# A decoder step of two layers: diagonal squares of 16, turned values through DRAM, halves on GpSimd

## The chip, the core and the metric

One core of a Trainium2 chip runs one program: TensorE (PE, with its weight loads PEld), VectorE (DVE), ScalarE (ACT), GpSimd (POOL) and SyncE (SP, which issues all DMAs of this kernel). The metric is device microseconds of one execution, lower is better. All arithmetic is in float32, or in float32 split into a high and a low half of a faster matmul type (fp32r).

## The reference

One step of a hybrid recurrent decoder with two layers, on 1024 prompt tokens and 8 sample rows, with model width 1024. Each layer normalises `x`, projects it with one wide weight matrix, mixes along time, and projects back:

```python
h = RMSNorm(x) * (1 + scale) + shift          # scale, shift, gate from silu(c) @ ada_w + ada_b
proj = h @ w_in
# even layer: 8 heads of gated DeltaNet (DK = DV = 128) beside 8 heads of mLSTM
#   o_a solves, per chunk, (I + A) U = rhs with A strictly lower triangular
# odd layer: 4 heads of GLA beside 4 heads of retention (DK = 128, DV = 256), per chunk:
#   o     = (q * decay) @ S + att @ v          # att: masked, decayed q k^T
#   S_new = decay * S + (k * decay)^T @ v
y = concat(branch outputs) * silu(z)
x = x + gate * (y @ w_out)
```

After both layers comes a plain RMSNorm. Outputs are `y` of both groups and the final states.

## The kernel before

**Recording and planning.** The kernel does not run its instructions in the order of its code. `Recorder` takes each call as an `Op` with its queue, a cost (`_cost` for DVE, ACT and POOL, `_pe_cost` for PE) and its dependencies; `order` then plans all queues, forwards from the ranks of the code and backwards in turns, and `emit` issues each queue's instructions in that order. Every engine works in order, and SP too: a DMA that waits for something holds those behind it. `self.nc.after` adds a dependency to all that is recorded while it is set; `urgent` puts what it encloses earlier. All instructions carry the line of `emit`, L451, in the profile, so they are told apart by their tiles.

**Layout.** Activations lie with features on partitions and 1032 tokens (1024 and 8) along the free side, in `slot` buffers with fixed names (`s_kd`, `s_vs`, `s_EM`, `s_pt` and so on in the profile). Small things lie in one `arena` that the even and the odd layer use in turn, from the same offsets. Weights come 128 columns at a time (`load_w`: 512 KB into `wf`, two buffers) and `halves` splits them: ACT writes `whi`, DVE writes the difference `wlo`. A projection of one such tile is 3 token blocks x 8 row tiles x 3 products (high x high, high x low, low x high), 72 matmuls of 344 columns.

**Even layer.** For each of eight heads, `gdn_proj` projects k, v, z and q, `gdn_mix` turns and scales them and walks over eight chunks of 128 tokens, and a generator of the mLSTM heads is advanced in between. For each head `inverse` computes the inverse of eight unit triangular matrices of 128x128 (the chunks'): it sends the diagonal 32x32 blocks through DRAM (`nd`), so that all diagonal 8x8 squares lie on 128 partitions, substitutes there in seven steps of two DVE operations, sends the result back through DRAM (`yd`) as blocks of 32 (`D`), and doubles twice: from 8 to 16 and from 16 to 32. Each doubling has two blocks of 32 small matmuls (8 chunks x 4 partition groups), a masking operation by `icode` between them, a subtraction and a DVE transpose. Doublings from 32 to 64 and to 128 follow. `even_setup` lays down `icode`, the unit squares `i8` and zeros in `yd`.

**Between the layers.** `out_proj` multiplies the 16 tiles of y by the output weights; `split` loads a y tile from DRAM (`yd`) into a staging slot and makes its halves, on ACT and then on DVE or POOL. The last two, 14 and 15, are split after the first output columns have been begun on the other 14. `odd_setup` loads the odd layer's constants (`lmask`, `rdm`, `rin`, `rend`, `w2`, `cosT`, `sinT`).

**Odd layer.** For each of four heads: `gla_proj`, `gla_mix`, `ret_proj`, `ret_mix`. Both mixes need keys and values with tokens on partitions. `by_token` turns one 128x1024 tile with 16 DVE transposes of 32x256, each from one group of 32 partitions to another; `v_tokens` does that for the two value tiles of a head (into `s_kd` and `s_vs`), and each mix does it once more for its keys (into `s_N`). `chunks256` then walks over the eight chunks: per chunk the values are weights of two matmuls against `aT` and the moving side of two against the keys. `finish256` squares and norms the result (a small sum through `rd` in DRAM, back on all partitions), multiplies by the gate on DVE and by the norm on POOL, and stores y. After the last head, `out_proj` runs once more and ends in the final norm.

Of the kernel before, what the change touches and what calls it, by code (L numbers as in the profile page):

```python
# [9 lines left out]
F32 = mybir.dt.float32  # L10
F32R = mybir.dt.float32r
AF = mybir.ActivationFunctionType
ALU = mybir.AluOpType
# [4 lines left out]
T = 1024  # L18
# [6 lines left out]
NC = T // L  # L25
# [14 lines left out]
def host_constants():  # L40
    f = np.float32
    c = {}
    c["ident"] = np.eye(128, dtype=f)
    pos = np.concatenate([np.arange(T), np.full(NS, 8192)]).astype(f)
    inv = (f(10000.0) ** (-np.arange(64, dtype=f) / f(64))).astype(f)
    ang = (pos[None, :] * inv[:, None]).astype(f).astype(np.float64)
    c["cosT"] = np.concatenate([np.cos(ang), np.cos(ang)], 0).astype(f)
    c["sinT"] = np.concatenate([np.sin(ang), -np.sin(ang)], 0).astype(f)
    lg = np.log(1.0 - 2.0 ** (-5.0 - np.arange(4)))
    s, t = np.arange(L)[:, None], np.arange(L)[None, :]  # L50
    dm = np.zeros((L, 4, L))
    for h in range(4):
        dm[:, h, :] = np.where(t >= s, np.exp(lg[h] * np.maximum(t - s, 0)), 0.0)
    c["rdm"] = dm.astype(f).reshape(L, 4 * L)
    inn = np.exp(lg[:, None] * (np.arange(L)[None, :] + 1.0))
    c["rin"] = np.broadcast_to(inn[None], (128, 4, L)).astype(f).reshape(128, 4 * L).copy()
    c["rend"] = np.exp(lg[None, :] * (L - 1.0 - np.arange(L)[:, None])).astype(f)
    lm = np.zeros((32, 6, 32), f)
    ss, tt = np.arange(32)[:, None], np.arange(32)[None, :]
    for i, m in enumerate((16, 8, 4, 2, 1)):  # L60
        lm[:, i, :] = (ss // (2 * m) == tt // (2 * m)) & (ss % (2 * m) < m) & (tt % (2 * m) >= m)
    lm[:, 5, :] = ss == tt
    c["lmask"] = np.tile(lm, (4, 1, 1)).reshape(128, 192).copy()

    code = np.zeros((32, 32), f)
    for i in range(2):
        code[lm[:, 1 - i, :].T > 0] = 1.0 + i
    c["icode"] = np.tile(code, (4, 1))
    c["i8"] = np.tile(np.eye(8, dtype=f).reshape(1, 64), (128, 1))

    sel = np.zeros((2, 4, 8, 4, 32), f)
    for to, at in enumerate((1, 0, 2, 3)):
        for i in range(8):
            sel[:, at, i, to, i] = 1.0
    c["sel"] = sel.reshape(64, 128)
    return c
# [32 lines left out]
def _cost(queue, method, out, args, kw):  # L109

    n, sbuf, psum, scalars = _operands(out, args, kw)
    if queue == "scalar":
        return (165 + 0.84 * n if psum else 207 + 0.832 * n) + 60 * (scalars > 0) + 60 * ("accum_out" in kw), False
    if queue == "vector":
        if method == "tensor_reduce":
            return 150 + 1.042 * _elems(args[1]), False
        if method == "reciprocal":
            return 150 + 6.25 * n, False
        if method == "transpose":
            return 436.0, False  # L120
        if method == "tensor_tensor_scan":
            return 160 + 2.083 * n, True
        if method == "memset":
            return 65 + 0.52 * n, False
        if method in ("tensor_copy", "tensor_scalar") and not psum:
            return 152 + 0.57 * n + 45 * (scalars > 0), True
        return 153 + 1.042 * n + 57 * (scalars > 0), not psum
    if queue == "gpsimd":
        if kw.get("op") == ALU.pow:
            return 150 + 186.0 * n, True  # L130
        if method == "memset":
            return 100 + 0.83 * n, False
        if method == "tensor_copy":
            return 100 + 1.12 * n, True
        return (195 + 2.15 * n if method == "tensor_tensor" else 250 + 0.83 * n), True
    return 0.0, False


def _pe_cost(method, out, args, kw):
# [3 lines left out]
    n, rows, cols = _elems(kw["rhs"]), kw["lhsT"].shape[0], kw["lhsT"].shape[1]  # L143
    if kw["rhs"].dtype == F32R:
        return 0.45 * n + 2.5, "pass"
    if kw.get("tile_position") is not None and cols <= 32:
        return (max(1.87 * n / 4, 15.0) if rows > 32 else 15.0), (rows, cols)
    if rows <= 64 and cols <= 64:
        return max(1.67 * n + 9, 117.0), (rows, cols)
    kind = "whole" if rows == 128 and (cols == 128 or kw.get("tile_position") is None) else (rows, cols)  # L150
# [316 lines left out]
class Step:  # L467
# [428 lines left out]
    def halves(self, w, n=KT):  # L896
        hi, lo = (self.wtile(x, [128, KT, 128])[:, 0:n] for x in ("whi", "wlo"))
        self.act(hi, w[:, 0:n], AF.Copy)
        self.nc.vector.tensor_tensor(lo, w[:, 0:n], hi, op=ALU.subtract)
        return hi, lo  # L900

    def proj_parts(self, parts, ks):
# [390 lines left out]
    def inverse(self, N):  # L1293
# [3 lines left out]
        nd, yd = (self.nyd[x][self.turn(x, 2)] for x in ("nd", "yd"))  # L1297
        by32 = lambda x, j: x.rearrange("(c j q) x -> c j (q x)", c=NC, j=4)[:, j, 0:1024].rearrange(
            "c (s t) -> s c t", t=32)
        by8 = lambda x: x[:, 0:256].rearrange("m (r t) -> m r t", t=32)[:, :, 0:8]  # L1300
        blocks = [slice(32 * j, 32 * j + 32) for j in range(4)]
        for j, b in enumerate(blocks):
            dma(by32(nd, j), N[b, :, b])
        n8, y8, t8 = (self.const([128, 8, 8], x) for x in ("n8", "y8", "t8"))
        dma(n8, by8(nd))
        G.tensor_copy(y8, self.i8)
        for s in range(7):
            n = 7 - s
            V.tensor_tensor(t8[:, 0:s + 1, 0:n], y8[:, 0:s + 1, s:s + 1].to_broadcast([128, s + 1, n]),
                            n8[:, s:s + 1, s + 1:8].to_broadcast([128, s + 1, n]), op=ALU.mult)  # L1310
            V.tensor_tensor(y8[:, 0:s + 1, s + 1:8], y8[:, 0:s + 1, s + 1:8], t8[:, 0:s + 1, 0:n], op=ALU.subtract)
        dma(by8(yd), y8)

        t = self.slot("EM", name="inv")
        D, At, qt, Dt = (t[:, 256 * i:256 * i + 256].rearrange("p (c t) -> p c t", c=NC) for i in range(4))
        for j, b in enumerate(blocks):
            dma(D[b], by32(yd, j))
        V.transpose(Dt, D)
        for i in range(1, 3):
            p = self.ps(None, [128, NC, 32])  # L1320
            for c in range(NC):
                for j, b in enumerate(blocks):
                    self.mm(p[b, c, :], N[b, c, b], Dt[b, c, :], tile_position=(32 * j, 32 * j))
            V.scalar_tensor_tensor(At, self.icode.unsqueeze(1).to_broadcast([128, NC, 32]), float(i), p,
                                   op0=ALU.is_equal, op1=ALU.mult)
            p = self.ps(None, [128, NC, 32])
            for c in range(NC):
                for j, b in enumerate(blocks):
                    self.mm(p[b, c, :], At[b, c, :], D[b, c, :], tile_position=(32 * j, 32 * j))
            V.tensor_tensor(D, D, p, op=ALU.subtract)  # L1330
            V.transpose(Dt, D)
        Y = self.slot("Y", [128, NC, L], name="Y")
        G.memset(Y, 0.0)
        for b in blocks:
# [2 lines left out]
        p = self.ps(None, [128, 2, NC, 32])  # L1337
# [283 lines left out]
    def even_setup(self):  # L1621
        nc, a, V, G = self.nc, self.a, self.nc.vector, self.nc.gpsimd
        self.bkq = self.const([128, 258], "bkq")
        G.memset(self.bkq, 0.0)
        self.icode = self.const([128, 16], "icode").bitcast(mybir.dt.bfloat16)
        self.i8 = self.c_load("i8", [128, 8, 8])
        zero = self.slot("aT", [128, 264], name="zero")
        G.memset(zero, 0.0)
        for x in self.nyd["yd"]:
            self.nc.sync.dma_start(x, zero)  # L1630
        code = self.slot("EM", [128, 32], name="code")
        self.nc.sync.dma_start(code, self.a["icode"])
        self.nc.vector.tensor_copy(self.icode, code)
        self.vs = self.const([128, 2, NS], "mvs")
        self.ozs = self.const([128, 2, NS], "mozs")
        self.nms = self.const([128, 2, 2, NS], "mnms")
# [22 lines left out]

    def odd_setup(self):  # L1660
        nc, a = self.nc, self.a
        self.lmask = self.c_load("lmask", [128, 6, 32])
        self.rdm = self.c_load("rdm", [128, 4, L])
        self.rin = self.c_load("rin", [128, 4, L])
# [5 lines left out]
        nc.sync.dma_start(self.cosT, a["cosT"])  # L1670
        self.sinT = self.slot("mk", name="sinT")
        nc.sync.dma_start(self.sinT, a["sinT"])
        self.glr = self.slot("va", name="glr")
        self.qk_w = [self.load_w(a["od_w_in"][0], c) for c in (0, 512)]

# [32 lines left out]
    def by_token(self, out, x):  # L1708

        x = x[:, 0:T].rearrange("p (c t) -> p c t", t=L)  # L1710
        for i in range(0, 128, 32):
            for j in range(0, 128, 32):
                self.nc.vector.transpose(out[j:j + 32, :, i:i + 32], x[i:i + 32, :, j:j + 32])

    def v_tokens(self, v):
        vt = []
        for i, tag in enumerate(("kd", "vs")):
            t = self.slot(tag, [128, NC, 128], name="vt")
            self.by_token(t, v[i])
            vt.append(t)  # L1720
        return vt

    def chunks256(self, aT, qg, kt, vt, decay, out):

# [222 lines left out]
    def out_proj(self, src, l, mod):  # L1947
# [45 lines left out]
        def x_in(n):  # L1993
            x = xs[n % 2] if last else self.x_slot(n)
            nc.sync.dma_start(x, self.xd[l][n])
            return x
# [57 lines left out]
            G.tensor_tensor(wl[:, 1], w, wl[:, 0], op=ALU.subtract)  # L2054
        for k in late:
            split(k)
        x2 = [x_in(n) for n in range(2)]
        for n in range(2):
            for j in range(3):
# [61 lines left out]
    def build(self):  # L2121
        tc, nc = self.tc, self.nc
        with ExitStack() as ctx:
# [20 lines left out]
            self.sd = [dr.tile([16, 128], F32, name=f"sd{i}") for i in range(2)]  # L2144
            self.spd = dr.tile([16, W], F32, name="spd")
            self.rd = [dr.tile([4, QB], F32, name=f"rd{i}") for i in range(2)]
            self.nyd = {x: [dr.tile([128, 264], F32, name=f"{x}{i}") for i in range(2)] for x in ("nd", "yd")}
            self.program()
            with tc.manual_schedule():
                self.nc.emit()  # L2150
# [103 lines left out]
```

## Time and profile before

| | |
|---|---|
| median of three runs | 2292.83 us (2287.20 to 2294.88) |
| the profiled execution | 2289.05 us, its span 2287.0 us |
| mean granted clock of PE | 0.987 |
| busy: PE, DVE, ACT, POOL | 2221.4, 1382.8, 747.7, 527.7 us |
| moved by DMA | 235.20 MB |

The span is the time from the first to the last instruction of the program in the profiled execution; the time of the execution has 2.05 us more around it. A busy time is the union of an engine's instructions, so matmuls that overlap in the pipeline count once. The even layer's heads run until about 1160 us, the odd layer's projections begin at about 1400 us, and the last output projection ends the span.

### The profile page before, as it was taken

The page shows a single profiled execution, that of the slowest core. Times are in us where ns is not written, and L with a number is a line of the kernel's source. Part 1 is how long each engine was busy: PE and PEld are TensorE (multiplying, and loading weights), DVE is VectorE, ACT ScalarE, POOL GpSimd, SP SyncE. Part 2 cuts the span into 40 slices and gives each one's busy share as a digit, 9 for nine tenths or more (in the row PEclk, how much of TensorE's full clock was granted, in tenths as well). Part 3 has the DMA queues.
Part 4 walks back from the last instruction along what each step waited for, and adds up shares of the span by engine and source line. Part 5 has one row for each costly group of instructions (what it writes and reads, how often), then busy time and mean ns, then how long its engine had stood idle before and what let it go on. Part 6 is the DMA issues. An engine that isn't in the chain of part 4 may idle for free.

```text
span 2287.0 us, 44726 instructions
## 1 busy us (share of the span) xinstructions
PE 2221.4 (97%) x18844; PEld 2070.0 (91%) x18844; DVE 1382.8 (60%) x2700; ACT 747.7 (33%) x1374; POOL 527.7 (23%) x385
## 2 busy tenths in 40 slices
PE   6999999999999999999989999999999999998998
PEld 5777788899999999899989999999999999997997
DVE  6774646565564646556453355876976876977332
ACT  4422323232233233232331134234225324334322
POOL 3121112111123012211330031422422422433100
PEclk8999999999999999999999999999999999998999
DMA  9362544422143212432362221233142143246222
GB/s 260 124 165 60 152 133 121 129 77 72 40 118 105 69 52 86 108 95 72 114 216 84 75 76 38 56 122 107 43 136 94 50 133 95 56 149 209 74 58 91
DMA packets 285455, 235.20 MB, mean 103 GB/s; under 512 B 47819, under 2 KB 257733, under 8 KB 285246
## 3 DMA queue, kind: packets, MB, share of 16 engines
q1 hardware_dynamic: 285254, 232.35, 34.6%
q8 instruction: 147, 2.41, 0.4%
q14 instruction: 54, 0.44, 0.1%
HBM read 185.59 MB, written 46.91 MB: 102 GB/s over the span
## 4 chain that ended last, share of the span: by engine, by line
PE 88%; DMA 4%; DVE 4%; issue 1%; ACT 1%; POOL 1%; SPq 1%; POOLq 0%; DVEq 0%; ACTq 0%
PE pj L451 68%; PE A L451 14%; PE B L451 6%; DMA wf<-in_ev_w_in 1%; SPq L451 1%; DMA s_aT<-rd 0%; DVE s_h L451 0%; DMA s_h<-in_x_prompt 0%; DVE arena L451 0%; DVE s_N L451 0%; DMA s_pt<-yd 0%; DVE s_pt L451 0%; DMA ed<-s_Y 0%; DMA s_mp<-gd 0%; DVE s_mp L451 0%
## 5 line engine op out<-in xcount | busy, mean ns | idle before, releaser
L451 PE MATMUL pj<-s_h,whi 128*128 128x344 f32 (+1 forms) x6024 | 1498.6, 327 | 10.8 <-ACT s_h L451 5.4
L451 PEld LDWEIGHTS pj<-s_h,whi 128*128 128x128 f32 (+1 forms) x6024 | 1042.7, 189 | 44.8 <-issue 25.3
L451 PE MATMUL pj<-s_h,wlo 128*128 128x344 f32 (+1 forms) x3024 | 982.2, 325 | 1.5 <-DVE wlo L451 0.9
L451 PEld LDWEIGHTS pj<-s_h,wlo 128*128 128x128 f32 (+1 forms) x3024 | 569.8, 189 | 16.1 <-issue 10.6
L451 DVE TENSOR_TENSOR wlo<-wf,whi 128x1024 fp32r<-128x1024 f32 (+1 forms) x144 | 192.9, 1340 | 291.2 <-ACT whi L451 272.3
L451 ACT ACTIVATE whi<-wf 128x1024 fp32r<-128x1024 f32 (+2 forms) x146 | 152.1, 1043 | 374.9 <-PE pj L451 330.3
L451 ACT ACTIVATE s_pt<-pj 128x344 f32<-128x344 f32 (+1 forms) x170 | 77.0, 453 | 288.3 <-PE pj L451 282.8
L451 POOL TENSOR_TENSOR arena<-arena,base 128x8 f32<-128x8 f32 (+5 forms) x38 | 64.4, 1697 | 377.8 <-DVE arena L451 377.1
L451 POOL TENSOR_TENSOR s_tmp<-s_EM 128x512 f32<-128x512 f32 (+1 forms) x60 | 88.5, 1493 | 156.2 <-PE A L451 69.1
L451 DVE SCALAR_TENSOR_TENSOR s_pt<-s_u,base,s_pt 128x1024 f32<-128x1024 f32 x72 | 96.5, 1341 | 0.3
L451 ACT ACTIVATE s_u<-pj 128x344 f32<-128x344 f32 x93 | 41.9, 453 | 142.4 <-PE pj L451 80.2
L451 DVE SCALAR_TENSOR_TENSOR arena<-arena,A 128x128 f32<-128x128 f32 (+1 forms) x84 | 32.8, 391 | 84.5 <-PE A L451 83.9
L451 DVE STREAM_TRANSPOSE s_kd<-s_u 32x256 f32<-32x256 f32 x128 | 55.8, 436 | 16.6 <-ACT s_u L451 13.5
L451 POOL TENSOR_TENSOR s_tmp<-s_tmp,arena 128x1024 f32<-128x1024 f32 (+2 forms) x26 | 43.4, 1676 | 88.6 <-PE A L451 62.2
L451 POOL TENSOR_TENSOR s_kd<-s_kd,s_vs 128x1032 f32<-128x1032 f32 x8 | 21.5, 2688 | 167.6 <-ACT s_vs L451 152.2
L451 DVE SCALAR_TENSOR_TENSOR s_zz<-s_pt,pj 128x344 f32<-128x344 f32 x96 | 48.4, 507 | 18.7 <-ACT s_pt L451 17.9
L451 DVE STREAM_TRANSPOSE s_vs<-s_v 32x256 f32<-32x256 f32 x128 | 55.8, 436 | 1.9
L451 ACT ACTIVATE arena<-A,arena 128x128 f32<-128x128 f32 x64 | 23.5, 368 | 100.8 <-PE A L451 100.5
L451 ACT ACTIVATE s_tmp<-s_tmp 128x1024 f32<-128x1024 f32 (+1 forms) x44 | 46.1, 1054 | 28.7 <-POOL s_tmp L451 24.0
L451 DVE SCALAR_TENSOR_TENSOR arena<-arena,B 64x130 f32<-64x130 f32 (+1 forms) x84 | 31.2, 371 | 38.6 <-PE B L451 37.2
L451 ACT ACT_TABLE_LOAD x41 | 52.6, 1283 | 5.2 <-DMA s_h<-in_x_prompt 4.5
L451 POOL MEMSET s_u<- 128x3 f32 x24 | 2.4, 101 | 208.5 <-DVE s_pt L451 208.5
(643 smaller groups left out, 3597.7 us busy)
## 6 DMA issues: line engine op xcount, KB each, us to landing
wf<-in_ev_w_in SPq DMA_DIRECT2D x64, 512.0 KB
wf<-in_od_w_in SPq DMA_DIRECT2D x48, 512.0 KB
wf<-in_ada_w SPq DMA_DIRECT2D x32, 512.0 KB
s_pt<-yd SPq DMA_DIRECT2D x24, 516.0 KB
s_tmp<-sd SPq DMA_DIRECT2D x24, 512.0 KB
yd<-s_qg SPq DMA_DIRECT2D x15, 516.0 KB
wf<-in_ev_w_out SPq DMA_DIRECT2D x14, 512.0 KB
wf<-in_od_w_out SPq DMA_DIRECT2D x14, 512.0 KB
```

The costliest lines, as they stand in the source:

```text
L451: op.fn(*[self.placed(x) for x in op.args], **{k: self.placed(x) for k, x in op.kw.items()})
```

## The change

The diff has six parts.

1. `inverse` substitutes in squares of 16 on 64 partitions (15 steps of two DVE operations), and one doubling is left of the two. The unit squares come from DRAM (`i16`) for each head; rows of `nd` and `yd` are 528 long, so that diagonal squares of 16 start at regular places. The squares lie in the slot `EM` and no longer in the arena, and `imask` takes the place of `icode`.
2. `v_tokens` no longer calls `by_token`. The new `squares` turns a value tile with one DVE transpose in squares of 32x32, written with a step of eight elements, stores the tile to DRAM (`td`, 512 KB), and loads it back in four transfers that put each square in the right partition group. The tile's free side then is (feature, chunk), so `vt[x][:, c, :]` has a step of eight elements (32 bytes).
3. `halves` in the odd layer sends every second difference `wlo` to GpSimd.
4. The loads of constants in `odd_setup` depend on `split_at`, the last operation of the last `split` in the even layer's `out_proj`.
5. The planner's cost of a DVE transpose grows with its size (it was 436 ns for each), and that of a small tiled matmul changes.
6. `even_setup` follows part 1.

```diff
@@ _cost, _pe_cost @@
         if method == "transpose":
-            return 436.0, False
+            return 100 + 1.31 * n, False
...
     if kw.get("tile_position") is not None and cols <= 32:
-        return (max(1.87 * n / 4, 15.0) if rows > 32 else 15.0), (rows, cols)
+        return (max(0.8 * n, 20.0) if rows > 32 else 18.0), (rows, cols)
@@ halves @@
-        self.nc.vector.tensor_tensor(lo, w[:, 0:n], hi, op=ALU.subtract)
+        (self.nc.gpsimd if self.layer == "odd" and self.turn("half", 2) else self.nc.vector).tensor_tensor(lo, w[:, 0:n], hi, op=ALU.subtract)
@@ inverse @@
+        t = self.slot("EM", name="inv")
+        D, At, qt, Dt = (t[:, 256 * i:256 * i + 256].rearrange("p (c t) -> p c t", c=NC) for i in range(4))
+        nb, yb, tb = (t[0:64, 256 * i:256 * i + 256].rearrange("p (r t) -> p r t", t=16) for i in (1, 2, 3))
+        dma(yb, self.a["i16"].rearrange("p (r t) -> p r t", t=16))
         for j, b in enumerate(blocks):
             dma(by32(nd, j), N[b, :, b])
-        dma(n8, by8(nd))
-        G.tensor_copy(y8, self.i8)
-        for s in range(7):
+        dma(nb, by16(nd))
+        for s in range(15):
...
-        for i in range(1, 3):
-            p = self.ps(None, [128, NC, 32])
-            for c in range(NC):
-                for j, b in enumerate(blocks):
-                    self.mm(p[b, c, :], N[b, c, b], Dt[b, c, :], tile_position=(32 * j, 32 * j))
-            V.scalar_tensor_tensor(At, self.icode.unsqueeze(1).to_broadcast([128, NC, 32]), float(i), p,
-                                   op0=ALU.is_equal, op1=ALU.mult)
...
+        p = self.ps(None, [128, NC, 32])
+        for c in range(NC):
+            for j, b in enumerate(blocks):
+                self.mm(p[b, c, :], N[b, c, b], Dt[b, c, :], tile_position=(32 * j, 32 * j))
+        V.tensor_tensor(At, p, self.imask.unsqueeze(1).to_broadcast([128, NC, 32]), op=ALU.mult)
...
@@ odd_setup @@
+        self.nc.after = (self.split_at,)
         self.lmask = self.c_load("lmask", [128, 6, 32])
...
         nc.sync.dma_start(self.sinT, a["sinT"])
+        self.nc.after = ()
@@ squares, v_tokens @@
+    def squares(self, y, x):
+        dma = self.nc.sync.dma_start
+        y = y[:, 0:T]
+        self.nc.vector.transpose(y.rearrange("p (b j c) -> p b c j", b=4, c=NC),
+                                 x[:, 0:T].rearrange("p (c b i) -> p b c i", b=4, c=NC))
+        d = self.td[self.turn("td", 4)]
+        dma(d, y)
+        for b in range(4):
+            dma(y[32 * b:32 * b + 32].rearrange("i (a x) -> i a x", a=4),
+                d.rearrange("(a i) (b x) -> b i a x", a=4, b=4)[b])
+        return y.rearrange("p (d c) -> p c d", c=NC)
+
     def v_tokens(self, v):
-        vt = []
-        for i, tag in enumerate(("kd", "vs")):
-            t = self.slot(tag, [128, NC, 128], name="vt")
-            self.by_token(t, v[i])
-            vt.append(t)
-        return vt
+        return [self.squares(self.slot(tag, name="vt"), v[i]) for i, tag in enumerate(("kd", "vs"))]
@@ out_proj @@
         for k in late:
             split(k)
+        self.split_at = len(self.nc.ops) - 1
@@ build @@
-            self.nyd = {x: [dr.tile([128, 264], F32, name=f"{x}{i}") for i in range(2)] for x in ("nd", "yd")}
+            self.td = [dr.tile([128, T], F32, name=f"td{i}") for i in range(4)]
+            self.nyd = {x: [dr.tile([64, 528], F32, name=f"{x}{i}") for i in range(2)] for x in ("nd", "yd")}
```

More of the change, by code (lines that the diff above doesn't have):

```diff
@@ L63, in host_constants @@
     c["lmask"] = np.tile(lm, (4, 1, 1)).reshape(128, 192).copy()
[L65 to L69, printed above, removed]
+    c["imask"] = np.tile(lm[:, 0, :].T, (4, 1)).copy()
+    c["i16"] = np.tile(np.eye(16, dtype=f).reshape(1, 256), (64, 1))
     sel = np.zeros((2, 4, 8, 4, 32), f)
@@ L1299, in inverse @@
             "c (s t) -> s c t", t=32)
-        by8 = lambda x: x[:, 0:256].rearrange("m (r t) -> m r t", t=32)[:, :, 0:8]
+        by16 = lambda x: x[:, 0:512].rearrange("m (r t) -> m r t", t=32)[:, :, 0:16]
         blocks = [slice(32 * j, 32 * j + 32) for j in range(4)]
+        t = self.slot("EM", name="inv")
+        D, At, qt, Dt = (t[:, 256 * i:256 * i + 256].rearrange("p (c t) -> p c t", c=NC) for i in range(4))
+        nb, yb, tb = (t[0:64, 256 * i:256 * i + 256].rearrange("p (r t) -> p r t", t=16) for i in (1, 2, 3))
+        dma(yb, self.a["i16"].rearrange("p (r t) -> p r t", t=16))
         for j, b in enumerate(blocks):
             dma(by32(nd, j), N[b, :, b])
-        n8, y8, t8 = (self.const([128, 8, 8], x) for x in ("n8", "y8", "t8"))
-        dma(n8, by8(nd))
-        G.tensor_copy(y8, self.i8)
-        for s in range(7):
[L1308 to L1315, printed above, removed]
+        dma(nb, by16(nd))
+        for s in range(15):
+            n = 15 - s
+            V.tensor_tensor(tb[:, 0:s + 1, 0:n], yb[:, 0:s + 1, s:s + 1].to_broadcast([64, s + 1, n]),
+                            nb[:, s:s + 1, s + 1:16].to_broadcast([64, s + 1, n]), op=ALU.mult)
+            V.tensor_tensor(yb[:, 0:s + 1, s + 1:16], yb[:, 0:s + 1, s + 1:16], tb[:, 0:s + 1, 0:n], op=ALU.subtract)
+        dma(by16(yd), yb)
         for j, b in enumerate(blocks):
@@ L1318, in inverse @@
         V.transpose(Dt, D)
-        for i in range(1, 3):
-            p = self.ps(None, [128, NC, 32])
-            for c in range(NC):
-                for j, b in enumerate(blocks):
-                    self.mm(p[b, c, :], N[b, c, b], Dt[b, c, :], tile_position=(32 * j, 32 * j))
-            V.scalar_tensor_tensor(At, self.icode.unsqueeze(1).to_broadcast([128, NC, 32]), float(i), p,
-                                   op0=ALU.is_equal, op1=ALU.mult)
[L1326 to L1331, printed above, removed]
+        p = self.ps(None, [128, NC, 32])
[3 more added lines that the diff above has]
+        V.tensor_tensor(At, p, self.imask.unsqueeze(1).to_broadcast([128, NC, 32]), op=ALU.mult)
+        p = self.ps(None, [128, NC, 32])
+        for c in range(NC):
+            for j, b in enumerate(blocks):
+                self.mm(p[b, c, :], At[b, c, :], D[b, c, :], tile_position=(32 * j, 32 * j))
+        V.tensor_tensor(D, D, p, op=ALU.subtract)
+        V.transpose(Dt, D)
         Y = self.slot("Y", [128, NC, L], name="Y")
@@ L1624, in even_setup @@
         G.memset(self.bkq, 0.0)
-        self.icode = self.const([128, 16], "icode").bitcast(mybir.dt.bfloat16)
-        self.i8 = self.c_load("i8", [128, 8, 8])
+        self.imask = self.const([128, 32], "imask")
+        self.nc.sync.dma_start(self.imask, self.a["imask"])
         zero = self.slot("aT", [128, 264], name="zero")
@@ L1629, in even_setup @@
         for x in self.nyd["yd"]:
[L1630 to L1633, printed above, removed]
+            self.nc.sync.dma_start(x.rearrange("m (a b) -> (m a) b", a=2), zero)
         self.vs = self.const([128, 2, NS], "mvs")
```

## The prediction

> **What bounds the kernel now.** I read the page first: the span, the busy shares, the chain of work that ended last by engine.
>
> ```profile
> span 2287.0 us, 44726 instructions
> PE 2221.4 (97%) x18844; PEld 2070.0 (91%) x18844; DVE 1382.8 (60%) x2700; ACT 747.7 (33%) x1374; POOL 527.7 (23%) x385
> PE 88%; DMA 4%; DVE 4%; issue 1%; ACT 1%; POOL 1%; SPq 1%; POOLq 0%; DVEq 0%; ACTq 0%
> ```
>
> TensorE (PE) is idle for 2287.0 - 2221.4 = 65.6 us of the span, and 88% of the chain is PE. So the time falls by what leaves PE, or by idle stretches that close; nothing else counts. Next the busy time by stretch (columns: stretch, its length, busy us of PE, PEld, DVE, ACT, POOL with instruction counts, granted PE clock, DMA share, GB/s): the heads of the even layer, the middle of the odd layer, and the two places where I found PE waiting behind the start.
>
> ```profile
> 500.00:1000.00 500.00, 496.99 (x4669) 470.15 (x4668) 285.20 (x669) 154.43 (x321) 109.64 (x84) 1.00 0.30 84
> 1600.00:1800.00 200.00, 199.85 (x1763) 191.76 (x1761) 156.83 (x259) 69.78 (x110) 62.11 (x35) 1.00 0.29 87
> 1172.00:1186.00 14.00, 7.17 (x30) 6.44 (x29) 10.56 (x8) 6.35 (x7) 5.89 (x3) 0.63 0.78 264
> 2056.00:2084.00 28.00, 18.16 (x92) 14.09 (x91) 26.29 (x48) 9.23 (x9) 13.51 (x6) 0.76 0.65 211
> ```
>
> In the even heads PE is busy 496.99 of 500 us, in the odd middle 199.85 of 200. DVE is busy 156.83 of 200 there, high but not the limit. In the turn between the layers (1172 to 1186) PE lost 14.00 - 7.17 = 6.8 us and ran at a mean granted clock of 0.63; at the odd layer's end (2056 to 2084) it lost 9.8 us, the clock was 0.76, and DVE was busy 26.29 of 28.
>
> **The change part by part.**
>
> *The inverse (eight even heads).* Two doubling steps, each two blocks of 32 small matmuls, become one. One block, among projection matmuls on PE's timeline (start, duration, what, count; a matmul of this type writes two records):
>
> ```profile
> 188.88 0.48 PE L451 MATMUL pj<-s_h,whi 128*128 128x344 f32 x2
> 189.28 0.75 PE L451 MATMUL A<-s_EM 32*32 32x32 f32 x64
> 189.97 0.42 PE L451 MATMUL pj<-s_h,wlo 128*128 128x344 f32 x1
> 190.23 0.48 PE L451 MATMUL pj<-s_h,whi 128*128 128x344 f32 x2
> 190.54 0.32 PE L451 MATMUL pj<-s_h,wlo 128*128 128x344 f32 x1
> 190.70 0.49 PE L451 MATMUL pj<-s_h,whi 128*128 128x344 f32 x2
> ```
>
> From 190.23 to 190.70 three projection matmuls start, so one takes 0.157 us. From 188.88 to 190.23 pass 1.35 us with three of them (0.47), so the block costs PE 0.88 us, the slow first matmul after it included. Two blocks times eight heads: 16 x 0.88 = 14.1 us. As PE is saturated there, I count all of it: **-14**.
>
> DVE loses and gains in the same chain:
>
> ```profile
> L451 DVE SCALAR_TENSOR_TENSOR s_EM<-arena,A 128x256 f32<-128x256 bf16 x16 | 6.7, 420 | 16.1 <-PE A L451 16.1
> L451 DVE TENSOR_TENSOR s_EM<-s_EM,A 128x256 f32<-128x256 f32 x16 | 6.7, 422 | 13.7 <-PE A L451 13.7
> L451 DVE STREAM_TRANSPOSE s_EM<-s_EM 128x256 f32<-128x256 f32 x24 | 10.6, 442 | 7.1 <-DMA s_EM<-yd 6.6
> L451 DVE TENSOR_TENSOR arena<-arena 128x15 f32<-128x15 f32 x32 | 5.6, 174 | 0.7
> L451 DVE TENSOR_TENSOR arena<-arena 128x7 f32<-128x7 f32 x32 | 5.4, 167 | 5.5 <-DMA arena<-nd 4.9
> ```
>
> A step removed saves 0.42 + 0.42 + 0.44 us of DVE and two blocks of 0.75 us, with their handoffs about 3 us of latency. The substitution in squares of 16 has 30 operations instead of 14, up to 64 elements a partition. From 167 ns at 7 and 174 at 15 elements, 1 ns an element gives 30 x 0.16 + 1.36 = 6.2 us against 14 x 0.16 + 0.17 = 2.4: +3.8. The head's chain is thus as long as before to 1 us, DVE gains 2.5 us a head (20 in all) in a layer where it is busy 285 of 500: nothing. If PE had no projections to fill in, each head would pay that 1 us, 8 in all. The reads and writes of the diagonal squares keep their count of runs (64 x 16 of 64 bytes for 128 x 8 of 32). The unit matrix now comes by a load of 64 KB per head, issued behind the exponentials' last use of the slot and ahead of the store of the squares; it has that store and a load back to hide in. The GpSimd copy that it replaces was off the path, and `imask` for `icode` costs nothing.
>
> *The turn of the values (odd layer).*
>
> ```profile
> L451 DVE STREAM_TRANSPOSE s_kd<-s_u 32x256 f32<-32x256 f32 x128 | 55.8, 436 | 16.6 <-ACT s_u L451 13.5 <-PE A L451 0.9
> L451 DVE STREAM_TRANSPOSE s_vs<-s_v 32x256 f32<-32x256 f32 x128 | 55.8, 436 | 1.9
> 2111.91 3.64 DMA s_aT<-rd
> 2049.93 7.77 DMA s_aT<-rd
> 1164.31 5.66 DMA s_pt<-yd
> ```
>
> It removes 256 x 0.436 = 111.6 us of DVE. Added are 16 transposes of 128x1024. No row shows one that stores with a step of 32 bytes: at the rate of these rows it is 4 x 0.436 = 1.74 us, and from the dense 128x256 row above as little as 4 x 0.442; twice for the step, 3.5, is my upper end. I take 1.74: 28 us. DVE falls by some 84 us off the path: **0** while PE is saturated. The keys' own 16 transposes a head stay.
>
> Then 16 x (one store of 512 KB, four loads of 128 KB): 80 issues on SP's queue, 16.8 MB. A 516 KB load takes 3.64 us in a calm queue and 7.77 in a full one, so a tile is ready after 1.7 + 3.6 to 7.8 + about the same again, 9 to 17 us, where 16 transposes took 7.0, both tiles 14. The values come two z-projections ahead of their use, except that in each head the slots `kd` and `vs` must be free. The reads wait in SP for the store's landing, up to 8 us, and the weight loads behind them wait too: a weight tile lasts 72 x 0.157 = 11.3 us on PE and there are two buffers, so a hold of 8 us with a load of 5.66 is still covered; 0, with 16 x 2 = 32 us if that cover were gone.
>
> The turned values now lie with a step of eight elements, and PE reads them so, 128 times as weights and 128 times as the moving side:
>
> ```profile
> 2028.08 0.38 PE L451 MATMUL A<-s_qg,arena 128*128 128x128 f32 x2
> 2028.30 0.39 PE L451 MATMUL A<-s_aT,s_kd 128*128 128x128 f32 x2
> 2028.53 0.39 PE L451 MATMUL A<-s_qg,arena 128*128 128x128 f32 x2
> ```
>
> Such a matmul takes 0.22 us now (2028.08, 2028.30, 2028.53), two records of 128 columns, 0.87 ns a column, where the projections read 344 columns in 157 ns, 0.46 ns each. So the port gives dense columns at nearly twice the rate that these ask for, and a step that halves the rate would be hidden on the moving side; of the weight side I have no faster row. No row reads with a step. Ends: 0, and +0.22 us for each of 256 = +57. I take **0**, nearest to the projections' row.
>
> [...]
>
> *Halves on GpSimd.* Of the odd layer's 62 weight tiles, 31 differences move.
>
> ```profile
> L451 DVE TENSOR_TENSOR wlo<-wf,whi 128x1024 fp32r<-128x1024 f32 x140 | 187.0, 1336 | 282.7 <-ACT whi L451 263.7 <-PE pj L451 12.1 <-ACT s_qg L451 4.7
> L451 POOL TENSOR_TENSOR s_tmp<-s_tmp,arena 128x1024 f32<-128x1024 f32 x20 | 38.0, 1901 | 79.8 <-PE A L451 62.2 <-PE B L451 17.5
> 2036.78 0.87 DVE L451 SCALAR_TENSOR_TENSOR s_tmp<-s_tmp,s_k,s_tmp 128x256 f32<-128x256 f32 x2
> 2038.44 2.69 POOL L451 TENSOR_TENSOR s_kd<-s_kd,s_vs 128x1032 f32<-128x1032 f32 x1 [17.86 <-ACT s_vs L451]
> 2038.77 3.04 DVE L451 SCALAR_TENSOR_TENSOR s_tmp<-s_tmp,s_k,s_tmp 128x256 f32<-128x256 f32 x2
> ```
>
> A difference gets 1901 - 1336 = 0.57 us longer, hidden in the 11.3 us of a tile. DVE's pair took 0.87 us alone and 3.04 beside GpSimd's operation: it stood still for 2.2 us, so DVE wins little. With all of it on the path: 31 x 0.57 = +17.5. I take 0.
>
> [...]
>
> *Odd constants behind `split_at`.* Eight loads move out of SP's queue at the turn between the layers, behind the last `split`.
>
> ```profile
> 1156.63 0.58 SPq L451 DMA_DIRECT2D arena<-in_rin  x1
> 1163.40 0.34 SPq L451 DMA_DIRECT2D arena<-in_lmask  x1
> 1163.83 0.85 SPq L451 DMA_DIRECT2D s_pt<-yd  x2
> 1177.73 1.23 PE L451 MATMUL pj<-s_h,whi 128*128 128x344 f32 x3 [5.42 <-ACT s_h L451]
> ```
>
> SP stood from 1157.21 to 1163.40 at `lmask`, whose place in the arena was still being stored from, with loads of y behind it; the first of them is on the chain (1164.31), and PE's gap of 5.42 us ends with the halves of such a y. The staging slots of those y's come free late too, by the differences on DVE and GpSimd, so not all 6 us come back. Ends: 0 and the 6.8 us of idle with the half clock on the 7.17 busy us (0.37 x 7.17 = 2.7), 9.5. I take 3: **-3**. What is late next is the differences of the y's on DVE. The constants are first used in the odd layer's mixes, after its first projections.
>
> *End of the odd layer.*
>
> ```profile
> 2047.34 4.02 DVE L451 STREAM_TRANSPOSE s_kd<-s_u 32x256 f32<-32x256 f32 x9
> 2061.32 4.04 DVE L451 STREAM_TRANSPOSE s_vs<-s_v 32x256 f32<-32x256 f32 x9
> 2064.32 4.36 DMA s_pt<-yd
> 2061.34 0.43 PE L451 MATMUL pj<-s_mq,whi 128*128 128x344 f32 x1 [2.87 <-DVE s_mq L451]
> 2066.14 0.38 PE L451 MATMUL B<-base,s_u 128*8 128x128 f32 x1 [2.99 <-DVE s_aT L451]
> ```
>
> Here DVE is the limit: between 2047 and 2065 it turns the last head's values (14 us, 3.5 in the new form) while PE waits for DVE twice, 2.87 and 2.99. Yet the chain runs beside it through a norm's load (7.77), GpSimd and the y load (4.36), which the change does not shorten, and the last value tile now makes a trip of 9 to 17 us. Ends: 0 and 9.8 idle plus 0.24 x 18.16 = 4.4 of clock, 14. I take **-4**, little more than one of the two waits.
>
> *New costs in the planner* add no instruction but give another order. PE has 3 us of idle in 500 to lose or win; 0, with 6 us either way.
>
> **Sum.** -14 - 3 - 4 = -21 us against the profiled execution's 2289.05 (span 2287.0 and 2 us around it). The median of the three runs, 2292.83, is 3.8 higher; from it I get **2272**.
>
> **The rivals.**
> 1. *PE pays for the step of 32 bytes* (slower). Place: `chunks256`. For it: the new layout, and that no row shows such a read. Against: fp32 columns are asked for at half the rate the port can give. Price: weights alone 128 x 0.22 = +28, both sides +57: 2300 to 2329. It decides from 21/256 = 0.08 us a matmul (no gain left), and is slower by over 0.3% (6.9 us, about what a measurement tells from no change) from 0.11.
> 2. *The halves on GpSimd come late.* GpSimd has pieces like that of 2.69 us ahead of a difference, DVE's stand-still on top; +17.5 with the stalls as forecast gives 2272 + 17.5 = 2289, no change. Against: 11.3 us a tile.
> 3. *Both stalls close.* -14 - 9.5 - 14 = -37.5: 2255. For it: DVE 26.29 of 28. Against: the DMA chain beside it.
> 4. *The named part alone does nothing*: the turn removes 84 us of DVE and PE sees none of it. That is in my sum already; without the stalls it leaves -14, 2279.
>
> **How the numbers follow.** Likeliest: sum as above, with rival 4 as its upper half, 0.52, own range 2264 to 2282. Rival 3: 0.12. Rival 2, or part of the inverse's gain lost: 0.18, a third of it still faster. Rival 1: 0.16, of it 0.03 no change and 0.13 slower; 0.02 slower otherwise. Faster 0.52 + 0.12 + 0.06 = 0.70; no change 0.12 + 0.03 = 0.15; slower 0.15. Range 2255 to 2296: rival 3's end below, rival 2's above; what is left out is mostly rival 1 (0.13) and a better end (0.06).
>
> **What would show it.** Small blocks on PE: 16 fewer of 0.88 us, and the even heads 14 us shorter. DVE in the odd layer down by about 100 us with PE's busy time there unchanged. A chunk matmul on values still 0.22 us after its predecessor: if 0.33 or 0.44, rival 1 has it. No wait of SP at `lmask`, and PE's gap near 1172 shorter than 5.42. PE's gaps with "POOL wlo" as releaser would speak for rival 2. I am wrong if PE's busy time does not fall by 10 to 18 us, or if new idle of over 10 us stands in the even heads.

## The result and the profile after

The changed kernel takes 2330.04 us (median, 2329.42 to 2333.17) against 2290.86 us for the kernel before on the same chip: a ratio of 1.0173 [1.0152, 1.0195], 39 us slower, where 2272 was predicted. It came out 1 us above the upper end of the first rival, PE paying for the step of 32 bytes (2300 to 2329).

The page after, its first lines (span; busy us of each engine) and its chain:

```profile
span 2327.0 us, 42748 instructions
PE 2268.4 (97%) x17820; PEld 2109.2 (91%) x17820; DVE 1285.7 (55%) x2531; ACT 748.0 (32%) x1374; POOL 594.6 (26%) x409
PE 87%; DVE 5%; DMA 4%; issue 1%; ACT 1%; SPq 0%; POOL 0%; POOLq 0%; DVEq 0%; ACTq 0%
```

PE has 1024 records fewer (the small blocks of the inverse) and is busy 47 us longer. Its idle time fell from 65.6 to 58.6 us. DVE lost 97 us (118 from 1400 us on, where some 100 were announced, less 20 more in the even heads), and the time did not see it. So the loss is work on PE, not a wait. The stretches of before, now. They stand at the same times as before; the last line is the stretch that matches 2056 to 2084, 42 us later, because the matmul that the prediction shows at 2061.34 (`pj<-s_mq,whi`) starts at 2103.4 now:

```profile
500.00:1000.00 500.00, 491.66 (x4161) 463.97 (x4160) 303.58 (x723) 153.35 (x322) 105.32 (x79) 1.00 0.32 84
1600.00:1800.00 200.00, 200.00 (x1619) 190.33 (x1618) 114.83 (x159) 68.89 (x107) 77.51 (x42) 0.99 0.36 110
1172.00:1186.00 14.00, 10.07 (x48) 9.63 (x49) 7.88 (x7) 5.94 (x6) 2.76 (x2) 0.76 0.78 279
2056.00:2084.00 28.00, 28.00 (x173) 27.04 (x172) 13.90 (x13) 12.72 (x20) 7.26 (x3) 1.00 0.48 157
2098.00:2126.00 28.00, 27.63 (x180) 26.10 (x180) 19.59 (x36) 15.14 (x17) 11.48 (x5) 1.00 0.78 259
```

In the odd middle (1600 to 1800) PE is full as before, but gets through 1619 records where it did 1763. That is the line to stop at: a busy share of 100% on both sides, and 8% fewer instructions in it.

Now the matmuls on values, by group (busy us, mean ns of one, idle before), first in the kernel before:

```profile
L451 PE MATMUL B<-s_vs,s_N 128*128 128x128 f32 x64 | 12.4, 275 | 0.0
L451 PE MATMUL A<-s_aT,s_vs 128*128 128x128 f32 x64 | 12.4, 275 | 0.0
L451 PEld LDWEIGHTS A<-s_aT,s_vs 128*128 128x128 f32 x64 | 9.9, 192 | 0.0
L451 PEld LDWEIGHTS B<-s_vs,s_N 128*128 128x128 f32 x64 | 9.7, 192 | 0.0
```

and after:

```profile
L448 PE MATMUL B<-s_vs,s_N 128*128 128x128 f32 x64 | 20.6, 412 | 0.0
L448 PE MATMUL A<-s_aT,s_vs 128*128 128x128 f32 x64 | 20.3, 399 | 0.0
L448 PEld LDWEIGHTS A<-s_aT,s_vs 128*128 128x128 f32 x64 | 17.8, 326 | 0.0
L448 PEld LDWEIGHTS B<-s_vs,s_N 128*128 128x128 f32 x64 | 13.3, 208 | 1.3
```

`s_aT,s_vs` has the values as weights: the load went from 192 to 326 ns. `s_vs,s_N` has them as the moving side, with dense keys as weights: its load stays near 192 (208), and the matmul itself went from 275 to 412. The rhythm on PE's timeline after (start, duration) gives the price:

```profile
1675.63 0.38 PE L448 MATMUL A<-s_qg,arena 128*128 128x128 f32 x2
1675.85 0.64 PE L448 MATMUL A<-s_aT,s_kd 128*128 128x128 f32 x2
1676.32 0.39 PE L448 MATMUL A<-s_qg,arena 128*128 128x128 f32 x2
1676.54 0.64 PE L448 MATMUL A<-s_aT,s_vs 128*128 128x128 f32 x2
1677.02 0.62 PE L448 MATMUL A<-s_kd,s_N 128*128 128x128 f32 x2
1677.46 0.65 PE L448 MATMUL A<-s_vs,s_N 128*128 128x128 f32 x2
```

The dense matmul (`s_qg,arena`) still hands over after 0.22 us; values as weights take 0.47 to 0.48, values as the moving side 0.44. Over all 256 the median step from a matmul's start to the next start is 0.223 us before on both sides, and after 0.472 (weights) and 0.444 (moving): 128 x 0.249 + 128 x 0.221 = 60 us. (The means give 54 us, 0.217 to 0.457 and 0.195 to 0.379: behind the last value matmul of a chunk a projection follows, and that step grew less, from 0.143 to 0.279.)

The rest of the change, then, should be worth about 39 - 60 = -21 us. The experiments test both halves of that sentence.

### The profile page after: what moved, and what is told of

It reads as the page before. It is cut to its first block, busy times and chain, and to the rows that moved or that the text cites. A ratio compares the mean times of both kernels' runs of the same rounds, so it can differ in the third digit from the quotient of the medians.

```text
span 2327.0 us, 42748 instructions
## 1 busy us (share of the span) xinstructions
PE 2268.4 (97%) x17820; PEld 2109.2 (91%) x17820; DVE 1285.7 (55%) x2531; ACT 748.0 (32%) x1374; POOL 594.6 (26%) x409
## 4 chain that ended last, share of the span: by engine, by line
PE 87%; DVE 5%; DMA 4%; issue 1%; ACT 1%; SPq 0%; POOL 0%; POOLq 0%; DVEq 0%; ACTq 0%
PE pj L448 66%; PE A L448 15%; PE B L448 6%; DMA wf<-in_ev_w_in 1%; DMA wf<-in_ada_w 1%; DVE s_EM L448 1%; DVE s_tmp L448 1%; DVE wlo L448 1%; DVE arena L448 0%; DVE s_pt L448 0%; SPq L448 0%; DMA yd<-s_EM 0%; ACT s_h L448 0%; DVE s_Y L448 0%; DVE s_zz L448 0%
## 5 line engine op out<-in xcount | busy, mean ns | idle before, releaser
L448 PEld LDWEIGHTS pj<-s_h,whi 128*128 128x128 f32 (+1 forms) x6024 | 1043.9, 189 | 42.9 <-issue 23.1
L448 DVE TENSOR_TENSOR wlo<-wf,whi 128x1024 fp32r<-128x1024 f32 x112 | 145.2, 1296 | 265.7 <-ACT whi L448 242.8
L448 ACT ACTIVATE whi<-wf 128x1024 fp32r<-128x1024 f32 (+1 forms) x146 | 152.2, 1043 | 366.1 <-PE pj L448 320.0
L448 POOL TENSOR_TENSOR wlo<-wf,whi 128x1024 fp32r<-128x1024 f32 (+1 forms) x32 | 77.2, 2412 | 199.1 <-ACT whi L448 198.8
L448 DVE TENSOR_TENSOR s_EM<-s_EM 64x15 f32<-64x15 f32 (+7 forms) x240 | 49.3, 205 | 13.3 <-DMA s_EM<-nd 7.5
```

The lines of the kernel that those rows point to most:

```text
L448: op.fn(*[self.placed(x) for x in op.args], **{k: self.placed(x) for k, x in op.kw.items()})
```

## The experiments

Two theories stood. *The step*: PE pays 60 us for reading values with 32 bytes between elements, and all else gains some 20. *The trip*: the loss lies in the transfers through DRAM, in SP's waits or in the new plan, and the longer records only show it. Ratios are against the kernel before on the same chip. The latter's medians on these chips are 2286.6 to 2288.3 us.

**The step without the trip.** In the kernel before, `v_tokens` alone:

```diff
-            t = self.slot(tag, [128, NC, 128], name="vt")
+            t = self.slot(tag, name="vt")[:, 0:T].rearrange("p (d c) -> p c d", c=NC)
```

> The kernel before with one line changed: its 32 DVE transposes of the values write each tile as (feature, chunk), so that PE reads it with a step of 32 bytes; no trip through DRAM, nothing else of the change. Theory (PE pays for the step on both sides, 0.235 us for each of 256 matmuls): 2291 + 60 = 2351, 2340 to 2360, with about 405 ns a record of the moving reads and 320 ns a weight load on values. Rival (the loss is in the trip through DRAM, in SP's waits or in the new plan): within 10 us of 2291.

Measured: 2376.47 us, ratio 1.0390 [1.0372, 1.0409], 90 us slower. The page's PE line and groups of this kernel:

```profile
PE 2291.2 (96%) x18844; PEld 2132.2 (90%) x18844; DVE 1428.6 (60%) x2700; ACT 747.4 (31%) x1374; POOL 524.9 (22%) x385
```

```profile
L451 PE MATMUL B<-s_vs,s_N 128*128 128x128 f32 x64 | 20.6, 412 | 0.0
L451 PEld LDWEIGHTS A<-s_aT,s_vs 128*128 128x128 f32 x64 | 17.8, 326 | 0.1
L451 PE MATMUL B<-s_aT,s_kd 128*128 128x128 f32 x64 | 20.8, 408 | 6.1 <-DVE s_mp L451 6.1
L451 DVE STREAM_TRANSPOSE s_kd<-s_u 32x256 f32<-32x256 f32 x128 | 87.1, 680 | 17.2 <-ACT s_u L451 14.1 <-PE A L451 0.8
```

Same 412 and 326 ns as in the changed kernel, same steps of 0.472 and 0.444 us, with no transfer in sight: the trip falls as the cause. The 30 us over the expected 60 are a miss. DVE's small transposes pay for the step too (680 ns for 436, +61 us over both tiles), and PE's idle time rose from 65.6 to 84.1 us, some of it waiting for DVE in the chunks (6.1 us in the row above). The last 10 us, more busy PE than the 60, are not explained. The largest group of projections is busy 1498.9 us there for 1491.2, at a mean granted clock of 0.983 for 0.987, so part of them lies in matmuls that read no values.

**The trip without the step.** The changed kernel, with a turn whose squares keep runs of 32 elements; four stores and four loads a tile put the runs in place (the end of `squares`; the transposes and transfers ahead of it are left out here):

```diff
...
-        return y.rearrange("p (d c) -> p c d", c=NC)
+        v = y.rearrange("p (h d l) -> p h l d", h=NC // l, l=l)      # here l = 1
+        return [v[:, c // l, c % l] for c in range(NC)]
```

> The changed kernel with the values laid down dense: the DVE transpose writes runs of 32 elements, four stores and four loads a tile put the runs in place (runs of 128 bytes in the stores), and the chunk matmuls read 128 neighbouring elements. All else as in the change. Theory (the step alone costs): 2330 - 60 = 2270, 2262 to 2278. Rival (the trip, SP or the plan costs): 2322 to 2336, with the matmuls on values at 0.22 us.

Measured: 2272.24 us, ratio 0.9926 [0.9900, 0.9951]. Against the changed kernel's 1.0173 that is 0.0247 x 2290 = 57 us for the step. Its page's PE line and its groups:

```profile
PE 2207.4 (97%) x17820; PEld 2056.4 (91%) x17820; DVE 1276.4 (56%) x2531; ACT 748.0 (33%) x1374; POOL 593.5 (26%) x409
```

```profile
L448 PE MATMUL B<-s_vs,s_N 128*128 128x128 f32 x64 | 12.4, 275 | 0.0
L448 PEld LDWEIGHTS A<-s_aT,s_vs 128*128 128x128 f32 x64 | 9.7, 192 | 0.0
```

PE is busy 61 us less than in the changed kernel (2268.4), at the same number of records. The theory of the step holds in both directions.

**The old turn.** The changed kernel with the old `v_tokens`, so 32 small DVE transposes a head and no trip.

> The changed kernel with the 32 DVE transposes a head of the kernel before for the values: dense, no trip. What is left is the inverse, the halves, the constants behind the last split and the planner's costs. Theory: 2330 - 60 and some of the 17 us that closed at the end of the odd layer come back: 2270 to 2285. If the trip with dense values is worth nothing, this run equals the dense trip within 5 us; if the trip relieves DVE at the odd layer's end, it is 8 to 15 us above it.

Measured: 2274.64 us, 0.9946 [0.9926, 0.9965]; the dense trip is 2.4 us below it, inside the intervals. Both of its stretches at the odd layer's end, first this kernel's, then the dense trip's:

```profile
2040.00:2062.00 22.00, 14.66 (x91) 12.26 (x90) 21.46 (x41) 10.87 (x12) 11.83 (x6) 0.77 0.66 229
```

```profile
2040.00:2062.00 22.00, 21.95 (x155) 20.77 (x154) 16.01 (x33) 10.08 (x12) 6.66 (x3) 1.00 1.02 290
```

With the old turn PE loses 7.3 us there, beside a DVE that is busy 21.46 of 22; with the new one the stall is gone. The totals differ by less, 2.4 us; the account of the odd layer's end below says where some of the rest went.

**Where the price begins.** The same turn with chunks interleaved by four (a step of 16 bytes) and by two (8 bytes): `l = 4` and `l = 2` in the code above.

> The changed kernel with a step of 16 bytes in place of 32: four DVE transposes a tile (one for each chunk of four), runs of 512 bytes in the stores, chunks 0 to 3 and 4 to 7 interleaved by four elements. [...] Theory B, the price grows with the bytes stepped over: half of the 60 us, 2295 to 2305. Theory C, 32 bytes is the limit: 2265 to 2275, records of 275 ns.

> The changed kernel with a step of 8 bytes: two DVE transposes a tile, runs of 256 bytes in the stores, chunks interleaved in pairs. [...] Theory B, the neighbours must be dense and the price is the same for any step: 2322 to 2336, records of about 400 ns. [...]

Measured: 2326.86 us (1.0179 [1.0155, 1.0203]) at 16 bytes, 2268.30 us (0.9911 [0.9894, 0.9928]) at 8. Groups at 16 bytes, then at 8:

```profile
L448 PE MATMUL B<-s_vs,s_N 128*128 128x128 f32 x64 | 20.3, 407 | 0.0
L448 PEld LDWEIGHTS A<-s_aT,s_vs 128*128 128x128 f32 x64 | 17.5, 322 | 0.0
```

```profile
L448 PE MATMUL B<-s_vs,s_N 128*128 128x128 f32 x64 | 12.4, 275 | 0.0
L448 PEld LDWEIGHTS A<-s_aT,s_vs 128*128 128x128 f32 x64 | 10.2, 197 | 0.0
```

Sixteen bytes cost nearly what 32 do (median steps of 0.464 and 0.436 us for 0.472 and 0.444). Eight bytes cost 5 ns of a weight load and 6 to 12 ns of a step (0.235 and 0.229 us for 0.223), some 2 us in all, which the total does not show. So it is no price per byte stepped over, and neighbours need not touch. Nor is 32 bytes the limit. Of the four steps tried, 4 and 8 bytes are fast, 16 and 32 slow. So the limit lies somewhere above 8 and no higher than 16; no step between these two was run, and what sets it no run shows.

**The other parts, each alone on the kernel before.** The inverse (all of its hunks); the constants (`split_at`); the halves (one line); the planner's two costs.

> The kernel before with the inverse alone changed (squares of 16, one doubling less; values turned as before, dense). By the sum of the prediction: 2290 - 14 = 2276. By what the changed kernel's trace shows of the even layer, where the work that left PE turned into idle and only 1.6 us were gained: 2286 to 2290, with 10 us or more of new PE idle before 1165 us.

> The kernel before with the odd layer's constants held back behind the last split, nothing else. Prediction: -3; by the changed kernel's trace -1.5 to -3, with PE's gap in the turn between the layers at about 3.8 us in place of 5.4: 2286 to 2289, which the runs can hardly tell from no change. Rival: with the waits of SP elsewhere it is worth nothing, gap 5.4.

> The kernel before with every second difference of the odd layer's weight halves on GpSimd, nothing else. Prediction: 0 (end +17.5). Theory from the run without the turn (2274.6, of which inverse and constants would explain 3 to 5 us): this part is worth most of the rest, -6 to -10, because DVE is the limit where the last head's values are turned and the differences there moved off it: PE idle of 2056 to 2084 below 5 us in place of 9.8. Rival: nothing, 2286 to 2292.

> The kernel before with the planner's two new costs alone; no instruction added or removed. Prediction: 0, 6 us either way. Theory: worse by 5 to 11 us, 2293 to 2299, lost ahead of 1165 us. Rival: 2284 to 2292.

| alone | median us | ratio | us, ratio x 2288 | predicted |
|---|---|---|---|---|
| inverse | 2272.63 | 0.9934 [0.9919, 0.9949] | -15 | -14 |
| constants | 2285.99 | 0.9995 [0.9985, 1.0006] | -1 | -3 |
| halves | 2288.53 | 1.0007 [0.9998, 1.0016] | +2 | 0 |
| costs | 2283.17 | 0.9978 [0.9966, 0.9989] | -5 | 0, 6 either way |

The inverse is worth what the sum said. I had come to doubt it from the changed kernel's trace and expected 2286 to 2290: that reading was wrong, and the run says so. The halves are nothing, which also fells my idea that they explain the run with the old turn; that run's 2274.64 is no better than the inverse alone (2272.63). The parts do not add up: alone they make -15 - 1 + 2 - 5 = -19 us, together, in that run, -12 (0.0054 x 2288). The costs alone gained a little, where I expected a loss.

**What the planner's costs do.** What had misled me is where the even layer ends. The first matmul of its output projection (last two numbers: first and last start of three), in the kernel before, the changed one, the one with the inverse alone, the one with 8-byte steps, and the latter with the costs of before:

```profile
L451 PE MATMUL pj<-s_N,whi x3: 318/320/403, 1162.0 to 1168.8; 128*128 128x344 f32 x3
```

```profile
L448 PE MATMUL pj<-s_N,whi x3: 320/321/404, 1160.5 to 1167.3; 128*128 128x344 f32 x3
```

```profile
L448 PE MATMUL pj<-s_N,whi x3: 319/320/321, 1149.0 to 1156.5; 128*128 128x344 f32 x3
```

```profile
L448 PE MATMUL pj<-s_N,whi x3: 320/320/403, 1163.4 to 1170.2; 128*128 128x344 f32 x3
```

```profile
L448 PE MATMUL pj<-s_N,whi x3: 317/320/405, 1151.9 to 1159.5; 128*128 128x344 f32 x3
```

The inverse alone ends the even layer 13 us earlier; with the new costs that gain is gone at this place. The costs alone do the same: 7 us later than before at this matmul, while the rest of the span is 6 shorter (in the profiled execution, at 2289.83 us the longest of twelve). But the halves alone, which change no instruction of the even layer, move this matmul too, 5 us earlier, and the total stays. First the costs alone, then the halves alone:

```profile
L451 PE MATMUL pj<-s_N,whi x3: 320/322/403, 1168.8 to 1176.0; 128*128 128x344 f32 x3
```

```profile
L451 PE MATMUL pj<-s_N,whi x3: 318/320/403, 1157.2 to 1164.0; 128*128 128x344 f32 x3
```

So I restored the old costs in the 8-byte version (two constants), and then also put all halves back on DVE.

> The changed kernel with a step of 8 bytes and the planner's costs of the kernel before (a DVE transpose 436 ns whatever its size, small tiled matmuls 15 ns); the rest of the change as it is. Theory: the new costs give a worse order in the even layer, whose end (first matmul of its output projection) is at 1160 to 1163 us in every run with them and at 1149 where the inverse alone is changed; so 2255 to 2262 here and that matmul near 1149. Rival: the order that comes out moves by about 5 us with any edit, the costs as such are worth nothing: 2264 to 2274.

> As the run with the costs of before (step of 8 bytes), and all differences of the odd layer's weight halves on DVE again: what is left of the change is the inverse, the turn through DRAM in 8-byte steps and the constants behind the last split. If the halves on GpSimd are worth nothing (as alone, 2288.5 against 2287.6) it equals that run within 4 us; if they now help because the turn frees GpSimd's rival DVE, it is 5 us or more slower; if they hurt, faster. Candidate for the best version: 2254 to 2268.

Measured: 2264.98 us, 0.9896 [0.9881, 0.9912], and 2264.47 us, 0.9893 [0.9878, 0.9907]. The even layer's end did come 11.5 us earlier (1151.9 for 1163.4), but the total moved by 3 us only, and the intervals overlap with 0.9911. The windows around the odd layer's end, old costs first, new costs second (shifted by 11.5 us):

```profile
2040.00:2100.00 60.00, 54.49 (x348) 52.87 (x349) 34.83 (x50) 25.41 (x32) 25.03 (x10) 0.91 0.62 199
```

```profile
2051.50:2111.50 60.00, 60.00 (x422) 58.35 (x420) 31.69 (x49) 30.16 (x41) 24.50 (x11) 1.00 0.56 181
```

Most of what the old costs win in the even layer they lose here: 5.5 us of idle PE and a clock of 0.91. The new costs trade one end for the other; why the order flips so is open. The rival of this pair, that the costs are worth nothing in the end, is the nearer one, and the halves are worth nothing here too. The two versions have the lowest medians of all runs, 24 us below the kernel before and some 64 us below the changed one (0.0280 x 2290).

## Why the prediction was wrong

By its own steps:

- **The strided reads, taken as 0: wrong, and the whole of the miss.** Measured +57 us by the totals and 54 to 60 by the steps, the upper end of the range given for this term (+57). The step that failed is "the port gives dense columns at nearly twice the rate that these ask for, and a step that halves the rate would be hidden". The projections' 0.46 ns a column is the rate of another type on dense reads; it says nothing of a read with a step, and the trace of before had no row with one. The argument took a far row for a near one and settled the largest unknown of the sum on it. The strided moving reads took 0.444 us for 256 columns, 1.73 ns a column: twice the 0.87 of this matmul's own dense reads and nearly four times the projections' 0.46, so there was no slack that hid the step. Rival 1 was to leave no gain from 0.08 us a matmul; it was 0.235 by the medians. Two of the prediction's own signs said so: the step of 0.44 us, and PE's busy time, which was to fall by 10 to 18 us and rose by 47.
- **The weight side, "no faster row": also paid,** 0.249 us a matmul against 0.221 on the moving side.
- **The inverse, -14: right in number** (-15 alone), made up otherwise: alone it lowered PE's busy time by 22.8 us (2198.6 for 2221.4) and added 5.7 us of idle, which the sum had at nothing. Where the 9 us beyond 14 come from is not traced. The prediction's own alarm, new idle of over 10 us in the even heads, did go off in the changed kernel: from 114 to 1149 us PE is idle 24.9 us, for 11.6 before. But where the gain is there, with the inverse alone, it is 23.1, so the alarm was no test. Before, changed, inverse alone:

```profile
114.00:1149.00 1035.00, 1023.44 (x9347) 932.26 (x9346) 595.39 (x1371) 314.43 (x641) 210.70 (x165) 1.00 0.35 99
```

```profile
114.00:1149.00 1035.00, 1010.07 (x8295) 915.08 (x8294) 615.71 (x1473) 310.67 (x645) 210.83 (x159) 0.99 0.38 100
```

```profile
114.00:1149.00 1035.00, 1011.91 (x8382) 925.45 (x8381) 622.75 (x1478) 315.78 (x655) 219.98 (x160) 0.99 0.38 101
```

- **The constants, -3: right in kind, too small to measure.** PE's gap at the turn did shrink, from 5.42 us to 3.76 in the changed kernel (the idle time in the row) and to 3.68 with the constants alone:

```profile
1174.52 1.23 PE L448 MATMUL pj<-s_h,whi 128*128 128x344 f32 x3 [3.76 <-ACT s_h L448]
```

  But the time gained by that part alone is 1 us, from 3 us less to 1 us more by its interval.
- **The end of the odd layer, -4: the stall closed** (27.63 of 28 busy at a clock of 1.00 in its stretch of the changed kernel, for 18.16 at 0.76), rival 3's case. Whether that is worth the 14 us of its upper end is another matter: between the runs with the old turn and the new one lie 2.4 us (dense, l = 1) and 0.9946 - 0.9911 = 0.0035, 8 us (steps of 8 bytes, l = 2). Some of the dense trip's gain is hidden by the even layer, which ends 4.6 us later there than with the old turn, though nothing in its code differs. The first matmul of its output projection, old turn first, dense trip second:

```profile
L448 PE MATMUL pj<-s_N,whi x3: 320/320/403, 1157.6 to 1164.5; 128*128 128x344 f32 x3
```

```profile
L448 PE MATMUL pj<-s_N,whi x3: 320/320/403, 1162.2 to 1169.0; 128*128 128x344 f32 x3
```

  From there to the end of the span the old turn takes 2273.8 - 1157.6 = 1116.2 us and the dense trip 2270.0 - 1162.2 = 1107.8, 8.4 less. So -4 looks too small by about half (8 in its place); why the even layer's end moves is open.
- **The transpose of 128x1024, 1.74 us: mis-sized without consequence.**

```profile
L448 DVE STREAM_TRANSPOSE s_vs<-s_v 128x1024 f32<-128x1024 f32 x8 | 18.0, 2256 | 11.8 <-ACT s_v L448 11.8
L448 POOL TENSOR_TENSOR wlo<-wf,whi 128x1024 fp32r<-128x1024 f32 x30 | 73.4, 2448 | 198.2 <-ACT whi L448 198.0
```

  It takes 2.26 us with the step of 32 bytes, inside 1.74 to 3.5. DVE, busy 55% of the span, is 5% of the chain.
- **Halves on GpSimd, 0: right,** though a difference takes 2.45 us there and not 1.90 (the row above).
- **SP's waits and the trip, 0: right.** The dense trip is no slower than the old turn (2272.24 us for 2274.64). **Planner, 0 and 6 either way: right as a bound** (-5 alone).

Without the one term the sum of -21 comes out near: the same change measured 0.9926 with dense values and 0.9911 with steps of 8 bytes, -17 and -20 us. Part of that is luck: the four parts tried alone differ by 7 us from what they make together (-19 and -12), and the planner's costs gave -5 and the constants -1 where the sum had 0 and -3.

## What to carry to other kernels

A layout that spares one engine can be paid by every later reader of the tile, here by 256 matmuls of PE, 57 us in all: before values are left interleaved, count the matmuls that read them and price the step at both ends, as weights and as the moving side (0.249 and 0.221 us a matmul here). If chunks must be interleaved, interleave float32 values in pairs (8 bytes), which cost nothing measurable here (2268.30 us, for 2272.24 dense), and not by four (2326.86) or eight (2330.04). And where a term's two ends are far apart (here 0 and +57) and no row is near, the sign of the forecast hangs on it and not on the finer terms.

## What the hardware showed that I had not expected

- PE's reads of these values show two speeds at the four steps tried, not a slope: steps of 4 and 8 bytes give 0.22 to 0.24 us (medians) for a 128x128 float32 matmul, 16 and 32 bytes 0.44 to 0.47.
- A DVE transpose in squares over 128x1024 takes 1.24 us dense, not four times the 442 ns of 128x256. A line through these two rows, an estimate, gives 708 ns for a dense 128x512; with a step of 8 bytes in the stores that size takes 685 to 697, so no price is seen there. At 16 bytes a 128x256 takes 631 ns for 442, and at 32 bytes a 128x1024 takes 2.26 us for 1.24. Dense, 8 bytes, 16 bytes:

```profile
L448 DVE STREAM_TRANSPOSE s_vs<-s_v 128x1024 f32<-128x1024 f32 x8 | 9.9, 1240 | 17.2 <-ACT s_v L448 17.2
```

```profile
L448 DVE STREAM_TRANSPOSE s_kd<-s_u 128x512 f32<-128x512 f32 x16 | 10.8, 697 | 15.3 <-ACT s_u L448 12.7 <-issue 2.0 <-PE A L448 0.5
```

```profile
L448 DVE STREAM_TRANSPOSE s_vs<-s_v 128x256 f32<-128x256 f32 x32 | 18.2, 631 | 5.9 <-ACT s_v L448 5.5 <-issue 0.2
```
